# Group-norm tail of a chunked RWKV-7 scan as a stage of its own, its scaling on ScalarE, and 1/|kk|² as a scalar operand in the triangular inverse

## The chip, the cores and the metric

The kernel runs on one core of a Trainium2 chip. The core has five engines that each work through their own list of instructions in order and meet at semaphores: TensorE (PE in the profile, with its weight loads as PEld), VectorE (DVE), ScalarE (ACT), GpSimd (POOL), and SyncE (SP), which here issues most of the DMAs. The metric is the device time of one execution in microseconds (us); a value given for a kernel is the median of its runs.

## What is computed

One layer of a decoder trunk on 1024 tokens of width 1024, all in fp32: an RWKV-7 time mixing, a gated convolution branch and a cross-attention, merged by gates. The change touches the RWKV-7 branch alone. Cut to that branch:

```python
kk = (k * k_k).reshape(B, S, H, N)                 # 16 heads of 64
kk = kk / jnp.maximum(jnp.sqrt(jnp.sum(kk * kk, -1, keepdims=True)), 1e-12)
k = k * (1.0 + (a - 1.0) * k_a)
# for every token t, one state of 64 x 64 for each head:
#   sa = state @ (-kk_t)
#   state = state * decay_t + sa (x) (kk_t * a_t) + v_t (x) k_t
#   y_t = state @ r_t
wkv = wkv7_scan(r, decay, k, v, -kk, kk * a)
mu = jnp.mean(wkv, -1, keepdims=True)              # group norm: one group for each head
var = jnp.mean(jnp.square(wkv - mu), -1, keepdims=True)
wkv = (wkv - mu) * lax.rsqrt(var + 64e-5) * gn_g + gn_b
o_rwkv = wkv + jnp.sum(r * k * r_k, -1, keepdims=True) * v
y_rwkv = (o_rwkv * jax.nn.silu(rwkv_gate)) @ w_proj_rwkv
```

## The kernel before, in words

The scan runs in chunks of 64 tokens. Two heads share the 128 partitions, so there are eight head pairs j, and each goes through two halves e of 512 tokens: 16 **units** (j, e) of eight chunks each. Four generators in the program deal with a unit:

- `prep` makes the scaled operands of the unit (tiles ar and bk), the sums |kk|² (written to a DRAM buffer ssd) and the chunk matrices g, of which the 32 x 32 triangular blocks go to a DRAM buffer ud.
- `sub` inverts those triangles. It loads them as U and |kk|² as rb, takes the reciprocal of rb (L577), multiplies U by it on GpSimd (L581), and puts it on the diagonal of W (L580). Then come 31 steps of two VectorE instructions each: tm = W column x U row (L587) and W += tm (L590). W goes to DRAM (wd, L594) and comes back in another layout as wb (L603). Four transposes (L607) put it into the tile TT, two rounds of small matmuls with a copy by ScalarE behind each (L615, L619, L625, L629) complete the 64 x 64 inverses. TT has one buffer and the next chain reads it.
- `chain` is the recurrence. `g_pre` transposes bk and v (L640, L647) and makes three products with TT and g (L664, L666, L673) that ScalarE copies out (L642, L651, L675, L679, L680). Then for each chunk: a matmul with the state (L709), an add (L710), a matmul for the new state (L717) and two state updates (L720). After each four chunks follow L731, L733, L738 and the statistics of the group norm (bn_stats, L742).
- The **tail** stands at the end of `chain`: six small VectorE instructions on the statistics (L750 to L755), the reciprocal root on GpSimd (L114 and the power L118), subtraction of the mean and product with the root on VectorE (L760, L761), four PE transposes (L766), gain, bonus and gate (L768, L769) and a store (L771).

Beside these, PE makes the big input projections ("dense", L298: 48 matmuls of 128 x 512 for each block of 128 columns), and ScalarE and VectorE split each weight tile in a high and a low part (L123, L124 "wl"). `schedule` says which dense blocks and which generators run together, as a span of the stage for each: while chain (j, 0) runs, sub (j, 1) and prep (j+1, 0) do too. `mix` takes steps of them in turn, and a scheduler in the framework then sets the order of the instructions on each engine. That order, once built, is fixed. After the scan, from about 1040 us on, come convolution, attention and output projections, in which PE has no gaps to speak of.

Of the kernel before, what the change touches and what calls it, by code (L numbers as in the profile page):

```python
# [18 lines left out]
P = 128  # L19
# [4 lines left out]
HS = 512  # L24
C = 64
CPH = HS // C
NG = 4
SUBW = 3
GNW = 1
CHN = 23  # L30
NR = 32 // NG
# [31 lines left out]
def hybrid_kernel(ctx: ExitStack, tc: tile.TileContext, x: bass.AP, mem: bass.AP, wt: bass.AP,  # L63
                  vecs: bass.AP, wup: bass.AP, gfin: bass.AP, out: bass.AP):
    nc = tc.nc
    act, dve, pool, pe = nc.scalar, nc.vector, nc.gpsimd, nc.tensor
# [105 lines left out]
    for j in range(KT):  # L172
        last = j == KT - 1
        schedule.append(([("g", j)] + [fill.pop(0) for _ in range(3)] if last else [("k", j + 1), ("r", j + 1), ("g", j)],
                         [([("chain", j, 0)], 0.0, 1.0), ([("sub", j, 1)], 0.0, 0.9)]
                         + ([] if last else [([("prep", j + 1, 0)], 0.35, 1.0)])))
        schedule.append(([fill.pop(0) for _ in range(2 + last)] + ([] if last else [("v", j + 1)]),
                         [([("chain", j, 1)], 0.0, 1.0)]
                         + ([] if last else [([("sub", j + 1, 0)], 0.0, 0.9), ([("prep", j + 1, 1)], 0.1, 0.9)])))
# [156 lines left out]
    with tc.tile_pool(name="rk", bufs=1, reuse_waits="tile") as rk:  # L336


        def so(par):
            return 0 if par else C  # L340
# [28 lines left out]
        TT = rk.tile([P, 8, C], F32, name="TT")  # L369
# [20 lines left out]
        def fl(ap):  # L390
            return ap.rearrange("p a t -> p (a t)")
# [73 lines left out]
        def g_prep(j, e):  # L465
# [98 lines left out]
        def g_sub(j, e):  # L564
            un = (2 * j + e) % 2
            g = GG[j, e]
            U = rk.tile([NG * 32, 32, 32], F32, name="U", tag="U", bufs=1)
            W = rk.tile([NG * 32, NR, 32], F32, name="W", tag="W")
            rb = rk.tile([NG * 32, 32], F32, name="rb", tag="rb", bufs=2)
            for q in range(NG):  # L570
                ps_ = slice(q * 32, (q + 1) * 32)
                nc.sync.dma_start(out=rb[ps_], in_=ssd[un].rearrange("b h c t -> (b h c) t"))
                nc.sync.dma_start(out=U[ps_], in_=ud[un].rearrange("b i s t -> (b i) s t"))
            pool.memset(W, 0.0)
            yield
            dve.tensor_scalar(out=rb, in0=rb, scalar1=1e-24, scalar2=None, op0=ALU.max)
            dve.reciprocal(out=rb, in_=rb)  # L577
            for q in range(NG):
                ps_ = slice(q * 32, (q + 1) * 32)
                pool.tensor_copy(fl(W[ps_])[:, q::32 + NG], rb[ps_, q::NG])  # L580
            pool.tensor_tensor(out=U, in0=U, in1=rb[:, None, :].broadcast_to([NG * 32, 32, 32]), op=ALU.mult)  # L581
            yield
            tm = rk.tile([NG * 32, max(-(-(i + 1) // NG) * (31 - i) for i in range(31))], F32, name="tm", tag="tm")
            for i in range(31):
                n, m = 31 - i, -(-(i + 1) // NG)
                tv = tm[:, 0:m * n].rearrange("p (a b) -> p a b", b=n)
                dve.tensor_tensor(out=tv, in0=W[:, 0:m, i:i + 1].broadcast_to([NG * 32, m, n]),  # L587
                                  in1=U[:, i:i + 1, i + 1:32].broadcast_to([NG * 32, m, n]), op=ALU.mult)
                wv_ = W[:, 0:m, i + 1:32]
                dve.tensor_tensor(out=wv_, in0=wv_, in1=tv, op=ALU.add)  # L590
                if i % 2:
                    yield
            for q in range(NG):
                nc.sync.dma_start(out=wd[un].rearrange("b i s t -> (b i) s t")[:, q::NG, :],  # L594
                                  in_=W[q * 32:(q + 1) * 32])

            wb = rk.tile([P, 8, 32], F32, name="wb", tag="wb")
            zt = rk.tile([P, 8, 32], F32, name="zt", tag="zt")
            for par in range(2):
                r0 = so(par)  # L600
                for b in range(2):
                    rows = slice(r0 + b * 32, r0 + (b + 1) * 32)
                    nc.sync.dma_start(out=wb[rows], in_=wd[un][b, par::2].rearrange("i s t -> s i t"))  # L603
            for par in range(2):
                for b in range(2):
                    rows = slice(so(par) + b * 32, so(par) + (b + 1) * 32)
                    dve.transpose(out=TT[rows, :, b * 32:(b + 1) * 32], in_=wb[rows])  # L607
            for _ in range(SUBW):
# [74 lines left out]
        def g_chain(j, e):  # L683
# [66 lines left out]
            dve.tensor_tensor(out=mn, in0=stv[:, :, 1], in1=stv[:, :, 4], op=ALU.add)  # L750
            dve.tensor_tensor(out=df, in0=stv[:, :, 1], in1=stv[:, :, 4], op=ALU.subtract)
            dve.tensor_scalar(out=mn, in0=mn, scalar1=0.5, scalar2=None, op0=ALU.mult)
            dve.tensor_tensor(out=vr, in0=stv[:, :, 2], in1=stv[:, :, 5], op=ALU.add)
            dve.tensor_tensor(out=df, in0=df, in1=df, op=ALU.mult)
            dve.scalar_tensor_tensor(out=vr, in0=df, scalar=16.0, in1=vr, op0=ALU.mult, op1=ALU.add)  # L755
            rsqrt(vr, vr, 1.0 / C, GN_EPS)
            for _ in range(GNW):
# [497 lines left out]
```

## Time and profile before

| | us |
|---|---|
| median of 3 runs | 1950.26 (1949.19 to 1952.72) |
| the profiled execution | 1949.77 |
| its span, first to last instruction | 1947.8 |
| PE busy | 1844.5 (95%) |
| DVE busy | 1410.6 (72%) |
| ACT busy | 691.9 (36%) |
| POOL busy | 227.7 (12%) |

Busy times are shares of the whole span, while the kernel has stages with different limits. In the profile's rows of 40 slices, PE is at 9 tenths nearly everywhere, DVE at 7 to 8 tenths in the first half (the scan) and at 9 in the convolution. A matmul's record is longer than the distance to the next matmul, so a busy PE hides small gaps. Instructions of one engine may overlap in their records by some tens of ns where they do not depend on each other.

### The profile page before, as it was taken

The page shows a single profiled execution, that of the slowest core. Times are in us where ns is not written, and L with a number is a line of the kernel's source. Part 1 is how long each engine was busy: PE and PEld are TensorE (multiplying, and loading weights), DVE is VectorE, ACT ScalarE, POOL GpSimd, SP SyncE. Part 2 cuts the span into 40 slices and gives each one's busy share as a digit, 9 for nine tenths or more (in the row PEclk, how much of TensorE's full clock was granted, in tenths as well). Part 3 has the DMA queues.
Part 4 walks back from the last instruction along what each step waited for, and adds up shares of the span by engine and source line. Part 5 has one row for each costly group of instructions (what it writes and reads, how often), then busy time and mean ns, then how long its engine had stood idle before and what let it go on. Part 6 is the DMA issues. An engine that isn't in the chain of part 4 may idle for free.

```text
span 1947.8 us, 30024 instructions
## 1 busy us (share of the span) xinstructions
PE 1844.5 (95%) x11412; PEld 1472.2 (76%) x11412; DVE 1410.6 (72%) x3028; ACT 691.9 (36%) x1303; POOL 227.7 (12%) x311
## 2 busy tenths in 40 slices
PE   6999998999899898998999999999999999899998
PEld 5777776766676676776788888888888788778886
DVE  5667787777878777787735998898999857654423
ACT  6334343433344343343333323131313335432121
POOL 2201111111111112111000000000000223100001
PEclk9999999999999999999999999999999999999999
DMA  4232212222121222212224411112122666785432
GB/s 147 57 99 58 77 35 63 60 56 74 42 83 44 62 63 53 77 42 71 69 72 141 130 54 55 65 59 71 44 76 87 227 199 214 246 283 170 129 130 86
DMA packets 127936, 188.61 MB, mean 97 GB/s; under 512 B 64432, under 2 KB 66608, under 8 KB 127792
## 3 DMA queue, kind: packets, MB, share of 16 engines
q1 hardware_dynamic: 122704, 178.11, 29.8%
q10 hardware_dynamic: 4768, 8.07, 1.1%
q8 instruction: 89, 1.46, 0.3%
q0 software_dynamic: 320, 0.52, 0.1%
q14 instruction: 55, 0.45, 0.1%
HBM read 139.92 MB, written 46.20 MB: 96 GB/s over the span
## 4 chain that ended last, share of the span: by engine, by line
PE 63%; DVE 23%; DMA 4%; issue 4%; ACT 3%; POOL 3%; SPq 0%; DVEq 0%; POOLq 0%; ACTq 0%
PE d L298 41%; PE g L298 5%; PE g L212 4%; DVE W L590 3%; DVE tm L587 3%; PE d L212 2%; DVE s L720 2%; PE g L552 2%; DVE wl L124 2%; DVE sav L710 1%; PE ry L894 1%; POOL vr L118 1%; DVE Y L761 1%; DVE Y L738 1%; PE sas L717 1%
## 5 line engine op out<-in xcount | busy, mean ns | idle before, releaser
L298 PE MATMUL d<-hH,wh 128*128 128x512 f32 x1504 | 607.2, 404 | 2.4 <-ACT lc L383 2.0
L298 PE MATMUL d<-hH,wl 128*128 128x512 f32 x1504 | 603.0, 401 | 0.0
L298 PE MATMUL d<-hL,wh 128*128 128x512 f32 x1504 | 600.1, 399 | 0.0
L298 PEld LDWEIGHTS d<-hH,wl 128*128 128x128 f32 x1504 | 285.0, 189 | 56.9
L298 PEld LDWEIGHTS d<-hH,wh 128*128 128x128 f32 x1504 | 285.3, 190 | 55.8 <-ACT lc L383 2.4
L298 PEld LDWEIGHTS d<-hL,wh 128*128 128x128 f32 x1504 | 285.0, 189 | 53.6
L848 DVE SCALAR_TENSOR_TENSOR ac<-up,wdw,ac 128x1024 f32<-128x1024 f32 x240 | 308.0, 1283 | 11.8 <-ACT ac L845 5.9
L123 ACT CAST wh<-wf 128x1024 fp32r<-128x1024 f32 x137 | 143.6, 1049 | 311.3 <-PE d L298 277.1
L124 DVE TENSOR_TENSOR wl<-wf,wh 128x1024 fp32r<-128x1024 f32 x137 | 177.6, 1296 | 83.8 <-ACT wh L123 83.3
L590 DVE TENSOR_TENSOR W<-W,tm 128x60 f32<-128x60 f32 (+24 forms) x496 | 112.3, 226 | 10.0
L587 DVE TENSOR_TENSOR tm<-W,U 128x60 f32<-128x60 f32 (+24 forms) x496 | 107.7, 217 | 11.1
L713 ACT ACTIVATE sp<-s,pc 128x128 f32<-128x128 f32 x120 | 48.3, 402 | 174.8 <-DVE s L720 137.6
L717 PEld LDWEIGHTS sas<-sav,tk 128*128 128x128 f32 x240 | 38.5, 188 | 67.7 <-DVE sav L710 49.4
L717 PE MATMUL sas<-sav,tk 128*128 128x128 f32 x240 | 54.2, 307 | 34.3 <-DVE sav L710 32.6
L720 DVE SCALAR_TENSOR_TENSOR s<-sas,pc,sp 64x64 f32<-64x64 f32 x240 | 67.6, 282 | 21.5 <-PE sas L717 16.1
L298 PE MATMUL g<-oH,wh 128*128 128x512 f32 x192 | 76.3, 398 | 5.3 <-ACT wh L123 5.3
L298 PE MATMUL g<-oH,wl 128*128 128x512 f32 x192 | 76.2, 397 | 2.1 <-DVE wl L124 2.1
L298 PE MATMUL g<-oL,wh 128*128 128x512 f32 x192 | 75.8, 395 | 0.0
L298 PE MATMUL d<-oL,wh 128*128 128x512 f32 x192 | 75.2, 392 | 0.0
L298 PE MATMUL d<-oH,wl 128*128 128x512 f32 x192 | 75.2, 392 | 0.0
L298 PE MATMUL d<-oH,wh 128*128 128x512 f32 x192 | 75.2, 392 | 0.0
L710 DVE TENSOR_TENSOR sav<-ry,Y 64x128 f32<-64x128 f32 x128 | 36.8, 287 | 43.7 <-ACT Y L675 26.8
(301 smaller groups left out, 2910.6 us busy)
## 6 DMA issues: line engine op xcount, KB each, us to landing
wf<-in_wt_dram SPq DMA_DIRECT2D x137, 512.0 KB
g_d<-gt SPq DMA_DIRECT2D x48, 256.0 KB
U<-ud SPq DMA_DIRECT2D x64, 128.0 KB
nxt<-in_x_dram SPq DMA_DIRECT2D x8, 512.0 KB
o_rwkv_d<-o SPq DMA_DIRECT2D x16, 256.0 KB
cv_d<-ac SPq DMA_DIRECT2D x8, 512.0 KB
o_mem_d<-om SPq DMA_DIRECT2D x16, 256.0 KB
xs<-cv_d SPq DMA_DIRECT2D x8, 512.0 KB
```

Of the source, the lines that this page charges most:

```text
L123: act.copy(hi, src)
L124: (eng or dve).tensor_tensor(out=lo, in0=src, in1=hi.bitcast(F32), op=ALU.subtract)
L212: pe.matmul(po, lhsT=l, rhs=r, start=(i == 0), stop=(i == n - 1))
L298: pe.matmul(po, lhsT=l[:, ks_], rhs=r[:, k, sl], start=(n == 0), stop=(n == 3 * KT - 1))
L552: pe.matmul(gps[hh][:, cc * P:(cc + 1) * P], lhsT=fl(bk[rows, c, :, :]), rhs=fl(ar[rows, c, :, :]), start=True, stop=True)
L587: dve.tensor_tensor(out=tv, in0=W[:, 0:m, i:i + 1].broadcast_to([NG * 32, m, n]), in1=U[:, i:i + 1, i + 1:32].broadcast_to([NG * 32, m, n] ...
L590: dve.tensor_tensor(out=wv_, in0=wv_, in1=tv, op=ALU.add)
L710: dve.tensor_tensor(out=sav[own, cc, :], in0=ry[own, cs], in1=Y[own, c // 2, :], op=ALU.add)
L713: act.activation(sp, S0, AF.Copy, scale=pc[:, c:c + 1])
L717: pe.matmul(sn[:, 0:P], lhsT=tk[:, cc, :], rhs=sav[:, cc, :], start=True, stop=True)
L720: dve.scalar_tensor_tensor(out=S1[vsl, vsl], in0=sn[vsl, vsl], scalar=pc[vsl, c:c + 1], in1=sp[vsl, vsl], op0=ALU.mult, op1=ALU.add)
L848: dve.scalar_tensor_tensor(out=ac, in0=up[:, tap:tap + S], scalar=wdw[:, tap * 8 + j:tap * 8 + j + 1], in1=ac, op0=ALU.mult, op1=ALU.add)
```

## The change

The tail leaves `chain` and becomes a generator `g_tail` that the schedule puts beside the *next* unit's chain, in the first half of its stage. The small arithmetic on the statistics moves from VectorE to GpSimd (eight small instructions beside the root), and the normalisation from two VectorE instructions over 128 x 512 to eight ScalarE instructions over 128 x 64 with a scale and a bias for each partition. Y, st and bv get two buffers, bk goes from three to two.

In `sub`, the diagonal of W is set to one by GpSimd, U stays as loaded, and 1/|kk|² enters each step as a scalar operand for each partition; one product at the end scales all of W. W gets two buffers. wb and zt now lie in U's buffer. One transpose over 128 partitions takes the place of four over 32, with two ScalarE copies for the part that it puts in the wrong column.

```diff
-    W = rk.tile([NG * 32, NR, 32], F32, name="W", tag="W")
+    W = rk.tile([NG * 32, NR, 32], F32, name="W", tag="W", bufs=2)
...
-        pool.tensor_copy(fl(W[ps_])[:, q::32 + NG], rb[ps_, q::NG])
-    pool.tensor_tensor(out=U, in0=U, in1=rb[:, None, :].broadcast_to([NG * 32, 32, 32]), op=ALU.mult)
+        pool.memset(fl(W[q * 32:(q + 1) * 32])[:, q::32 + NG], 1.0)
...
-        dve.tensor_tensor(out=tv, in0=W[...], in1=U[...], op=ALU.mult)
+        dve.scalar_tensor_tensor(out=tv, in0=W[...], scalar=rb[:, i:i + 1], in1=U[...], op0=ALU.mult, op1=ALU.mult)
...
+    dve.tensor_tensor(out=W, in0=W, in1=rb[:, None, :].broadcast_to([NG * 32, NR, 32]), op=ALU.mult)
...
-    wb = rk.tile([P, 8, 32], F32, name="wb", tag="wb")
-    zt = rk.tile([P, 8, 32], F32, name="zt", tag="zt")
+    wb, zt = U[:, 0:8, :], U[:, 8:16, :]
...
-            dve.transpose(out=TT[rows, :, b * 32:(b + 1) * 32], in_=wb[rows])     # 4 times
+    dve.transpose(out=TT[:, :, 0:32], in_=wb)
+        act.copy(TT[r1:r1 + 32, :, 32:C], TT[r1:r1 + 32, :, 0:32])               # 2 times
...
+def g_tail(j, e):
+    Y, st, bv = ENDS.pop((j, e))
...
-    dve.tensor_tensor(...)  six small ones on mn, df, vr
+    pool.tensor_tensor(...), pool.tensor_scalar(...)  eight small ones on mn, df, vr
     rsqrt(vr, vr, 1.0 / C, GN_EPS)
...
-    dve.tensor_tensor(out=yv, in0=yv, in1=mn[:, :, None].broadcast_to([P, n2, C]), op=ALU.subtract)
-    dve.tensor_tensor(out=yv, in0=yv, in1=vr[:, :, None].broadcast_to([P, n2, C]), op=ALU.mult)
+    for i in range(n2):
+        act.activation(yv[:, i, :], yv[:, i, :], AF.Identity, scale=vr[:, i:i + 1], bias=mn[:, i:i + 1])
```

Three places in the order of instructions, all around the start of chain (3, 1), show what this moves. Line numbers are those of the kernel that is shown. **ScalarE at the start of the chain**, before: zt and TT close the previous `sub`, then come the copies of `g_pre` (tk, sav, Y, tk, g).

```order
L629 COPY TT<-tr 32x8x32 x2
L733 COPY Y<-tr 128x256
L123 CAST wh<-wf 128x1024
L427 ACTIVATE sg<-d 128x512
L436 ACTIVATE gt<-d 128x512
L642 COPY tk<-tr 128x512
L651 COPY sav<-tr 64x2x128 x2
L675 COPY Y<-tr 128x256
L679 COPY tk<-g 64x2x128
```

And now, with the normalisation of the unit that has just ended (L768):

```order
L629 COPY TT<-tr 32x8x32 x2
L735 COPY Y<-tr 128x256
L643 COPY tk<-tr 128x512
L652 COPY sav<-tr 64x2x128 x2
L768 ACTIVATE Y<-Y,mn,vr 128x64 x3
L676 COPY Y<-tr 128x256
L680 COPY tk<-g 64x2x128
```

Three of the eight scalings of the old unit now stand ahead of the Y copy that the new chain's first add needs.

**VectorE at the start of the chain**, before:

```order
L760 TENSOR_TENSOR Y<-Y,mn 128x512
L428 SCALAR_TENSOR_TENSOR sg<-sg,d 128x512
L761 TENSOR_TENSOR Y<-Y,vr 128x512
L768 SCALAR_TENSOR_TENSOR o<-tr,vec,bv 128x512
L769 SCALAR_TENSOR_TENSOR o<-o,vec,sg 128x512
L710 TENSOR_TENSOR sav<-ry,Y 64x128
L587 TENSOR_TENSOR tm<-W,U 128x31
L590 TENSOR_TENSOR W<-W,tm 128x31
```

And now:

```order
L744 BN_STATS st<-Y 128x6 x4
L712 TENSOR_TENSOR sav<-ry,Y 64x128
L722 SCALAR_TENSOR_TENSOR s_0_405<-sas,pc,sp 64x64 x2
L488 TENSOR_SCALAR lw<-lw 128x512
L700 TENSOR_TENSOR bv<-g,v 128x512
L494 SCALAR_TENSOR_TENSOR lw<-rmask,lw 128x512
L712 TENSOR_TENSOR sav<-ry,Y 64x128
L586 SCALAR_TENSOR_TENSOR tm<-W,rb,U 128x31
L590 TENSOR_TENSOR W<-W,tm 128x31
```

The tail is gone from here, and the first of the 31 inverse steps stands behind the first state update where it stood ahead of it. (In the sub beside an even chain, (j, 0), the first step stood ahead even of the chain's first add.)

**VectorE between the last inverse step and the transposes**, in the sub beside chain (3, 0), whose result chain (3, 1) needs, before:

```order
L590 TENSOR_TENSOR W<-W,tm 128x8
L124 TENSOR_TENSOR wl<-wf,wh 128x1024
L720 SCALAR_TENSOR_TENSOR s_0_405<-sas,pc,sp 64x64 x2
L576 TENSOR_SCALAR rb<-rb 128x32
L124 TENSOR_TENSOR hsl<-rs,hsh 128x512
L710 TENSOR_TENSOR sav<-ry,Y 64x128
L577 RECIPROCAL rb<-rb 128x32
L555 TENSOR_TENSOR g<-g,cmask_384 128x512 x2
L720 SCALAR_TENSOR_TENSOR s_1_406<-sas,pc,sp 64x64 x2
L428 SCALAR_TENSOR_TENSOR sg<-sg,d 128x512
L607 STREAM_TRANSPOSE TT<-wb 32x8x32 x3
```

And now:

```order
L590 TENSOR_TENSOR W<-W,tm 128x8
L593 TENSOR_TENSOR W<-W,rb 128x256
L124 TENSOR_TENSOR wl<-wf,wh 128x1024
L429 SCALAR_TENSOR_TENSOR sg<-sg,d 128x512
L604 STREAM_TRANSPOSE TT<-U 128x8x32
```

The state updates, the masks of g (L555) and the head sums that stood behind the last step now stand ahead of it, between the steps.

## Rows read from the trace of the kernel before

**Rows 1.** Windows: us; busy (instructions) of PE, PEld, DVE, ACT, POOL; clock, DMA, GB/s.
```profile
520.80:636.30 115.50, 105.86 (x892) 80.53 (x890) 90.03 (x282) 45.35 (x98) 16.93 (x26) 1.00 0.22 59
1100.00:1200.00 100.00, 100.00 (x463) 83.44 (x462) 87.94 (x80) 25.98 (x33) 5.33 (x4) 1.00 0.22 69
```

**Rows 2.** Waits of PE over the span: us in total, times, longest.
```profile
PE sas L717 <- DVE sav L710: 32.6, 43, 1.9
PE tr L766 <- DVE Y L761: 19.1, 6, 3.2
```

**Rows 3.** Timeline, one tail: start us, us, instruction [idle before <-releaser].
```profile
529.55 0.69 DVE L760 TENSOR_TENSOR Y<-Y,mn 128x512 f32<-128x512 f32 x1
...
529.79 0.50 POOL L114 TENSOR_SCALAR vr<-vr 128x8 f32<-128x8 f32 x1 [11.90 <-DVE vr L755]
530.37 1.64 POOL L118 TENSOR_TENSOR vr<-vr,nhalf 128x8 f32<-128x8 f32 x1
531.98 2.34 POOL L581 TENSOR_TENSOR U<-U,rb 128x1024 f32<-128x1024 f32 x1
...
532.05 2.82 DVE L761 TENSOR_TENSOR Y<-Y,vr 128x512 f32<-128x512 f32 x1 [1.10 <-POOL vr L118]
...
535.01 0.63 PE L766 MATMUL tr<-ident,Y 128*128 128x128 f32 x4 [3.16 <-DVE Y L761]
```

**Rows 4.** Timeline of PE: the first, three in a row, the last L625 of sixteen.
```profile
127.16 0.69 PE L625 MATMUL tr<-zt,wb 32*32 32x32 f32 x32
...
523.52 0.69 PE L625 MATMUL tr<-zt,wb 32*32 32x32 f32 x32
...
584.61 0.69 PE L625 MATMUL tr<-zt,wb 32*32 32x32 f32 x32
...
637.39 0.69 PE L625 MATMUL tr<-zt,wb 32*32 32x32 f32 x32
...
980.64 0.69 PE L625 MATMUL tr<-zt,wb 32*32 32x32 f32 x32
```

**Rows 5.** Timeline of DVE: first and last step of one sub; second and last of the next.
```profile
540.72 0.19 DVE L587 TENSOR_TENSOR tm<-W,U 128x31 f32<-128x31 f32 x1
...
570.90 0.17 DVE L590 TENSOR_TENSOR W<-W,tm 128x8 f32<-128x8 f32 x1
...
594.46 0.18 DVE L587 TENSOR_TENSOR tm<-W,U 128x30 f32<-128x30 f32 x1
...
626.17 0.17 DVE L590 TENSOR_TENSOR W<-W,tm 128x8 f32<-128x8 f32 x1
```

**Rows 6.** Timeline of DVE: last inverse step, and transposes that wait for the data.
```profile
396.79 0.17 DVE L590 TENSOR_TENSOR W<-W,tm 128x8 f32<-128x8 f32 x1
...
405.24 0.90 DVE L607 STREAM_TRANSPOSE TT<-wb 32x256 f32<-32x256 f32 x2 [1.00 <-DMA wb<-wd]
```

**Rows 7.** Timeline: the start of chain (3, 1) on three engines.
```profile
527.29 0.60 DVE L742 BATCH_NORM_STATS2 st<-Y 128x6 f32<-128x64 f32 x4
...
539.99 0.37 ACT L675 COPY Y<-tr 128x256 f32<-128x256 f32 x1 [0.82 <-ACT sav L651]
...
540.84 0.46 PE L717 MATMUL sas<-sav,tk 128*128 128x128 f32 x2
```

**Rows 8.** Groups by line, 60 to 1040 us: busy us, mean ns | idle before.
```profile
L768 DVE SCALAR_TENSOR_TENSOR o<-tr,vec,bv 128x512 f32<-128x512 f32 x16 | 12.0, 750 | 7.0 <-PE tr L766 7.0
L698 DVE TENSOR_TENSOR bv<-g,v 128x512 f32<-128x512 f32 x16 | 11.1, 691 | 9.6 <-PE g L462 9.2
L555 DVE TENSOR_TENSOR g<-g,cmask 128x512 f32<-128x512 f32 x64 | 42.3, 687 | 19.0 <-PE g L552 18.6
L720 DVE SCALAR_TENSOR_TENSOR s<-sas,pc,sp 64x64 f32<-64x64 f32 x240 | 67.6, 282 | 21.5 <-PE sas L717 16.1
L713 ACT ACTIVATE sp<-s,pc 128x128 f32<-128x128 f32 x120 | 48.3, 402 | 174.8 <-DVE s L720 137.6 <-DVE s L687 36.5
L114 POOL TENSOR_SCALAR vr<-vr 128x8 f32<-128x8 f32 x16 | 4.9, 308 | 210.4 <-DVE vr L755 210.4
```

More of the change, by code (lines that the diff above doesn't have):

```diff
@@ L28 @@
 SUBW = 3
-GNW = 1
+GNW = 2
 CHN = 23
@@ L175, in hybrid_kernel @@
                          [([("chain", j, 0)], 0.0, 1.0), ([("sub", j, 1)], 0.0, 0.9)]
+                         + ([([("tail", j - 1, 1)], 0.0, 0.5)] if j else [])
                          + ([] if last else [([("prep", j + 1, 0)], 0.35, 1.0)])))
         schedule.append(([fill.pop(0) for _ in range(2 + last)] + ([] if last else [("v", j + 1)]),
-                         [([("chain", j, 1)], 0.0, 1.0)]
+                         [([("chain", j, 1)] + [("tail", j, 1)] * last, 0.0, 1.0), ([("tail", j, 0)], 0.0, 0.5)]
                          + ([] if last else [([("sub", j + 1, 0)], 0.0, 0.9), ([("prep", j + 1, 1)], 0.1, 0.9)])))
@@ L574, in g_sub @@
             pool.memset(W, 0.0)
+            for q in range(NG):
+                pool.memset(fl(W[q * 32:(q + 1) * 32])[:, q::32 + NG], 1.0)
             yield
@@ L586, in g_sub @@
                 tv = tm[:, 0:m * n].rearrange("p (a b) -> p a b", b=n)
-                dve.tensor_tensor(out=tv, in0=W[:, 0:m, i:i + 1].broadcast_to([NG * 32, m, n]),
-                                  in1=U[:, i:i + 1, i + 1:32].broadcast_to([NG * 32, m, n]), op=ALU.mult)
+                dve.scalar_tensor_tensor(out=tv, in0=W[:, 0:m, i:i + 1].broadcast_to([NG * 32, m, n]),
+                                         scalar=rb[:, i:i + 1], in1=U[:, i:i + 1, i + 1:32].broadcast_to([NG * 32, m, n]),
+                                         op0=ALU.mult, op1=ALU.mult)
                 wv_ = W[:, 0:m, i + 1:32]
@@ L603, in g_sub @@
                     nc.sync.dma_start(out=wb[rows], in_=wd[un][b, par::2].rearrange("i s t -> s i t"))
+            dve.transpose(out=TT[:, :, 0:32], in_=wb)
             for par in range(2):
-                for b in range(2):
-                    rows = slice(so(par) + b * 32, so(par) + (b + 1) * 32)
-                    dve.transpose(out=TT[rows, :, b * 32:(b + 1) * 32], in_=wb[rows])
+                r1 = so(par) + 32
+                act.copy(TT[r1:r1 + 32, :, 32:C], TT[r1:r1 + 32, :, 0:32])
             for _ in range(SUBW):
@@ L635, in hybrid_kernel @@
         state = [0]
+        ENDS = {}
         def g_pre(j, e, q, g, bk, v, Y):
@@ L749, in g_chain @@
             df = rk.tile([P, n2], F32, name="df", tag="df", bufs=1)
[L750 to L755, printed above, removed]
+            pool.tensor_tensor(out=mn, in0=stv[:, :, 1], in1=stv[:, :, 4], op=ALU.add)
+            pool.tensor_tensor(out=df, in0=stv[:, :, 1], in1=stv[:, :, 4], op=ALU.subtract)
+            pool.tensor_tensor(out=vr, in0=stv[:, :, 2], in1=stv[:, :, 5], op=ALU.add)
+            pool.tensor_tensor(out=df, in0=df, in1=df, op=ALU.mult)
+            pool.tensor_scalar(out=df, in0=df, scalar1=16.0, scalar2=None, op0=ALU.mult)
+            pool.tensor_tensor(out=vr, in0=vr, in1=df, op=ALU.add)
             rsqrt(vr, vr, 1.0 / C, GN_EPS)
+            pool.tensor_scalar(out=mn, in0=mn, scalar1=-0.5, scalar2=None, op0=ALU.mult)
+            pool.tensor_tensor(out=mn, in0=mn, in1=vr, op=ALU.mult)
             for _ in range(GNW):
@@ L759, in g_chain @@
             yv = Y.rearrange("p c (h v) -> p (c h) v", h=2)
-            dve.tensor_tensor(out=yv, in0=yv, in1=mn[:, :, None].broadcast_to([P, n2, C]), op=ALU.subtract)
-            dve.tensor_tensor(out=yv, in0=yv, in1=vr[:, :, None].broadcast_to([P, n2, C]), op=ALU.mult)
-            for _ in range(GNW):
-                yield
+            for i in range(n2):
+                act.activation(yv[:, i, :], yv[:, i, :], AF.Identity, scale=vr[:, i:i + 1], bias=mn[:, i:i + 1])
+                if i % 4 == 3:
+                    yield
             ytp = bank("tr")
@@ L775, in jobs @@
             return seq(*[tile_job(*a_) for a_ in lst])
-        n_steps = {"dense": 12, "prep": 13, "sub": 20 + SUBW, "chain": CHN + 2 * GNW}
-        make = {"prep": g_prep, "sub": g_sub, "chain": g_chain}
+        n_steps = {"dense": 12, "prep": 13, "sub": 20 + SUBW, "chain": CHN, "tail": 3 + GNW}
+        make = {"prep": g_prep, "sub": g_sub, "chain": g_chain, "tail": g_tail}
         for lst, work in schedule:
```

11 lines of the change are left out of this document (5 added, 6 removed).

## The prediction

> **What bounds the kernel now.** I read the windows first: 115.5 us in the middle of the scan (two units) and 100 us after it [rows 1]. After the scan PE does 463 instructions in 100 us with no gap, nearly all dense matmuls, so one costs 100/463 = 0.216 us. In the scan PE is busy 105.9 of 115.5 us, VectorE 90.0. Neither is full, so the stage is held by waits. Of PE's waits by releaser [rows 2] two matter: 19.1 us on the normalisation (six of 3.2 us at most), and 32.6 us in 43 short waits for the first add of a chunk.
>
> The timeline of one tail shows the first kind [rows 3]: L761 starts late, behind the root (1.64 us), takes 2.82 us beside the 2.34 us product of U on GpSimd, and PE stands 3.16 us ahead of the transposes L766, with the dense matmuls and the next chain's start queued behind. That is what the change removes.
>
> But what is this hidden by? A unit is a loop: inverse done (L625), chain starts, VectorE runs the next 31 steps, W goes through DRAM, L625 again. I count the scan in these intervals. From the first L625 to the last are 980.64 - 127.16 = 853.5 us, 15 of them, 56.9 each [rows 4]. Two in a row, 523.52 to 584.61 (61.1) and to 637.39 (52.8), split with the steps [rows 5] into three legs:
>
> - A, from L625 to the steps: 17.2 (540.72) in the first, 9.85 (594.46, the second step) in the second.
> - B, the steps to 571.07 and 626.34: 30.35 and 31.9.
> - C, from there to the next L625: 13.5 and 11.05.
>
> VectorE is back to back in B, so an instruction put there lengthens it, and its order is fixed. I take these legs for the bound, and ask what the change does to each.
>
> **Leg A.** The tail leaves the path, but something enters it. The statistics end 4.4 us after L625 (527.29 + 0.60 - 523.52, [rows 7]). Then GpSimd does eight small instructions, L114 and the power. For the small ones the nearest row is L114, 0.31 on the mean [rows 8] and 0.50 in the tail shown [rows 3]; a VectorE instruction as small, a bn_stats, takes 0.15 [rows 7], which is the lower end. With 0.31: 9 x 0.31 + 1.64 = 4.4, so they end at 8.8. As the order shows, three scalings of the old unit stand on ScalarE ahead of L675, which the new chain's first add needs. A 128 x 128 ScalarE instruction takes 0.40 [rows 8], which bounds the 128 x 64 one from above, half of that from below; I take 0.33, so 9.8. From the start of L675 to L717 are 0.85 [rows 7]: 10.7, with some 0.2 of semaphores 10.9. VectorE's first step now stands behind the first two state updates (2 x 0.28) and two large instructions or the second chunk's add: another 2.1. First step at 13.0 in both kinds. The first kind gains 4.2; the second, where the steps started ahead of the chain, loses 3.1. The ends for the small ones, 0.15 and 0.50, move A by -1.4 and +1.7.
>
> Does the small work on GpSimd disturb VectorE? L760, two operands from SBUF, took 0.69 while L114 ran beside it (0.50 in place of 0.31); L761 took 2.82 beside the 128 x 1024 product [rows 3]. So I take nothing for it.
>
> The Trainium skill, "GPSIMD Engine Reference", section 1 Specifications, states that GpSimd shares its SBUF interface with VectorE and contends with VectorE instructions that have two SBUF inputs. The large product agrees (2.82), the small L114 doesn't (0.69); by the rule the sum would be that of the fourth rival below, by the row it stays as it is.
>
> **Leg B.** Each step takes a scalar operand: the pointer form costs 0.750 against 0.691 of the plain product at the same size [rows 8], 0.06 each, 31 of them 1.9. The product that scales W is half of a 128 x 512 one, about 0.4. And the instructions that lay behind the last step or in the tail's place now stand between the steps. By the order of the first kind: two adds (0.28 each, as L720), L768 and L769 (0.75 each), two masks (0.69 each), two blends of the 0.75 form, less L698 and one of half a microsecond: 3.7. The sum is 6.0; neighbours that don't depend overlap by some tens of ns, so 5.5, and B is 36.0. In the second kind: four masks, two gates (0.69 each), one split (1.4), some small ones, less three blends and L698: 3.2; with 1.9 and 0.4 it is 5.5, and the first step, which now belongs to B, adds 0.4. B is 37.6. Lower end: VectorE absorbs the moved work in waits that the sum doesn't see, and only the 2.3 of the new product form stay: 32.6 and 34.5.
>
> **Leg C.** W's round trip through DRAM is 405.24 - 396.96 = 8.3 us [rows 6]. Behind it come one transpose (half of the 0.90 of two, 0.45), a round of small matmuls and a ScalarE copy: 10.5. PE's own queue has some 80 dense matmuls ahead of that round, 80 x 0.216 = 17.3, which began late since PE now waits at the chain's start; they may end a microsecond later. I take 11.0 for both. Little VectorE work is left here, so what left C is no gain beyond 2.5 in the first kind and nothing in the second. Two buffers for W only free GpSimd, which waits for nothing that anyone needs. U is loaded right after L625, since the wb in it is then free, and that is long ahead of 13.0.
>
> **The sum.** First kind 13.0 + 36.0 + 11.0 = 60.0; second 13.0 + 37.6 + 11.0 = 61.6. The order gives the first five intervals no such load, I leave them at 57; the last has a loop a fifth shorter, 52. Nine between at 60.6, a little under the mean of both: 285 + 545 + 52 = 882, +29. Behind the last L625 there are 51 fewer dense matmuls, -11.0, less 3 for the last unit's tail that nothing covers: -8. Two terms were taken at their full size, B's moved work and A's second kind; I take off 2. So +19 on the profiled 1949.8, which stands 0.5 under the median: **1969**.
>
> **The rivals.**
>
> - *PE is the bound.* The legs have slack that I don't see, VectorE takes its moved work in waits, and PE gets back its 19.1 us [rows 2] and the 11.0 at the end: 1920; with half of the 32.6 us of short waits 1904. For it: VectorE's total falls (L760, L761 and six small instructions against 2.3 + 0.4), and 90 of 115.5 leaves room. Against it: B is back to back. 0.28.
> - *Nothing net.* A's gain of 4.2 and C's of 2.5 in the first kind pay for B; intervals of 57.4 and 8 off the end: 1949 (1946 to 1953). 0.14.
> - *The chain waits for GpSimd longer.* The one place is the start of a chain, where three scalings stand ahead of L675. If the small instructions cost the 0.50 of rows 3, A grows by 1.7, over 15 units 25: 1994. It decides from about 0.4 each. Against it: VectorE has nothing to do then. 0.11.
> - *The small work on GpSimd slows VectorE* as the product did to L761, by 2.1 in 2.3 us. Then up to 4.4 us come back on VectorE for each unit, 15 x 4.4 = 66: 2035. Against it: L760 beside L114, and that VectorE waits then. 0.02.
> - *The change doesn't do what it says*, and the transposes still wait: L766 now stands behind the new chain's first products, some 5 us after the scalings, so no; inside the forecast.
>
> **How the numbers follow.** Forecast (1955 to 1985) 0.45, PE-bound 0.28, nothing 0.14, GpSimd's waits 0.11, its hold on VectorE 0.02. 0.2%, about 4 us, is what a measurement of this kernel can tell from no change. Faster 0.28, same 0.14, slower 0.58. The range, 1922 to 1996, leaves out the lower half of the PE-bound case and the far end above. The forecast's own range is 1955 to 1985.
>
> **What would show it.** L625 to L625 near 60 us in the middle of the scan against 57; the first step 13 us after L625; 36 us and more from first to last step; PE waiting no longer for the normalisation at L766, but ahead of L717 at the start of a chain and ahead of L615 for the round trip; ScalarE waiting for GpSimd right ahead of the scalings. If the first step comes by 10 us, or B stays at 32, the forecast is wrong and the PE-bound case right.

## The result, and the profile after

The changed kernel takes 1995.7 us (median of 4 runs, 1993.7 to 1997.3), the kernel before 1951.4: a ratio of 1.0241 with an interval of 1.0229 to 1.0253, 44 us slower. The forecast was slower, by 19. The time lies at the upper end of the range, and the loss is more than twice the forecast's. In the runs below, one execution of the kernel before, beside e13, took 2727.6 us at a granted clock of 0.61 and is left out of the ratio, and of e6 there is one execution alone.

The busy times of the changed kernel, from its page:

```profile
PE 1881.4 (94%) x11412; PEld 1512.6 (76%) x11412; DVE 1347.0 (67%) x2868; ACT 747.2 (37%) x1463; POOL 206.9 (10%) x423
```

VectorE has 64 us less to do than before (1410.6) and GpSimd 21 less, ScalarE 55 more. The time was not lost by work. Windows of the same 120 us in the middle of the scan, before and then after (us, busy us of PE, PEld, DVE, ACT, POOL with instructions, granted clock, DMA):

```profile
640.00:760.00 120.00, 110.28 (x867) 84.23 (x867) 93.25 (x294) 47.12 (x100) 17.76 (x28) 0.99 0.22 62
```

```profile
640.00:760.00 120.00, 109.98 (x818) 85.26 (x814) 71.58 (x231) 49.96 (x114) 12.96 (x38) 0.91 0.20 57
```

VectorE is busy for 22 us less, TensorE as long as before with fewer instructions, at a lower clock. Now the places that answer to [rows 4], the matmuls L625 of the changed kernel (start us, us): the first, three in a row, the last.

```profile
126.03 0.69 PE L625 MATMUL tr<-U 32*32 32x32 f32 x32
...
602.25 0.69 PE L625 MATMUL tr<-U 32*32 32x32 f32 x32
...
666.31 0.69 PE L625 MATMUL tr<-U 32*32 32x32 f32 x32
...
731.93 0.69 PE L625 MATMUL tr<-U 32*32 32x32 f32 x32
...
1036.78 0.69 PE L625 MATMUL tr<-U 32*32 32x32 f32 x32
```

From the first to the last are 910.8 us in place of 853.5: 57.3 lost here. Behind the last 958.7 are left of the span of 1995.5, before 967.2 of 1947.8: 8.5 won there. So the whole loss is in the fifteen intervals of the scan, as the prediction counted them.

TensorE's time in this whole stretch, from the first L625 to the last, before and then after:

```profile
127.16:980.64 853.48, 787.17 (x6317) 599.74 (x6317) 655.86 (x2054) 335.58 (x718) 121.95 (x183) 0.99 0.22 61
126.03:1036.78 910.75, 832.18 (x6368) 646.96 (x6368) 595.38 (x1915) 386.39 (x864) 100.06 (x275) 0.96 0.21 58
```

It is idle for 12.3 us more (78.6 for 66.3) and busy for 45.0 more. The 51 dense matmuls that the stretch has more are 11 us of this, at 0.216 each. And TensorE is busy for 75 us at a granted clock of 0.50, where it was 17: half of such time is lost, so 29 us more. This says where TensorE's time went; what would come back with the clock kept up, no run shows.

How one interval starts, from 666.31 on, answers to [rows 3, 7]:

```profile
670.83 0.21 POOL L754 TENSOR_TENSOR mn<-st 128x8 f32<-128x8 f32 x1 [12.14 <-DVE st L744]
...
672.84 1.67 POOL L118 TENSOR_TENSOR vr<-vr,nhalf 128x8 f32<-128x8 f32 x1
...
674.59 0.21 POOL L763 TENSOR_TENSOR mn<-mn,vr 128x8 f32<-128x8 f32 x1
674.83 1.10 ACT L768 ACTIVATE Y<-Y,mn,vr 128x64 f32<-128x64 f32 x3 [2.82 <-POOL mn L763]
675.95 0.37 ACT L676 COPY Y<-tr 128x256 f32<-128x256 f32 x1
...
676.38 0.44 PE L641 MATMUL tr<-ident,bk 128*128 128x128 f32 x2 [2.92 <-ACT Y L676]
...
676.80 0.46 PE L719 MATMUL sas<-sav,tk 128*128 128x128 f32 x2
...
677.30 0.77 PE L299 MATMUL d<-hH,wl 128*128 128x512 f32 x1
677.88 0.63 PE L299 MATMUL d<-hH,wh 128*128 128x512 f32 x1
...
680.00 0.24 DVE L586 SCALAR_TENSOR_TENSOR tm<-W,rb,U 128x31 f32<-128x31 f32 x1
```

GpSimd's small work ends 8.5 us after L625, ScalarE waits 2.82 us for it with the old unit's three scalings and the new chain's copy L676 behind, and TensorE stands 2.92 us at L641, which needs the bank (of PSUM, the memory that TensorE writes to) that this copy frees. Over the span these stalls are now TensorE's largest wait, and the tail's transposes (L773 here), 19.1 us in [rows 2], wait for 1.4:

```profile
PE tr L641 <- ACT Y L676: 32.2, 11, 3.0
PE ry L711 <- DVE s L722: 15.6, 19, 2.0
...
PE sas L719 <- DVE sav L712: 12.7, 18, 1.6
...
PE tr L773 <- ACT Y L768: 1.4, 4, 0.4
```

The stall at the tail is gone, and one about as long (2.92 us for 3.16) stands a few instructions on.

### The profile page after: what moved, and what is told of

The parts are those of the page before. It is cut to its first block, busy times and chain, and to the rows that moved or that the text cites. A ratio compares the mean times of both kernels' runs of the same rounds, so it can differ in the third digit from the quotient of the medians.

```text
span 1995.5 us, 30108 instructions
## 1 busy us (share of the span) xinstructions
PE 1881.4 (94%) x11412; PEld 1512.6 (76%) x11412; DVE 1347.0 (67%) x2868; ACT 747.2 (37%) x1463; POOL 206.9 (10%) x423
## 4 chain that ended last, share of the span: by engine, by line
PE 66%; DVE 19%; ACT 4%; POOL 4%; DMA 4%; issue 3%; DVEq 0%; POOLq 0%; SPq 0%; ACTq 0%
PE d L299 44%; PE g L299 5%; PE g L213 4%; DVE tm L586 3%; DVE W L590 2%; PE d L213 2%; DVE s L722 2%; PE g L553 2%; POOL vr L118 1%; DMA ost<-o_rwkv_d 1%; PE ry L901 1%; DVE wl L124 1%; PE sas L719 1%; PE ry L213 1%; DVE Y L740 1%
## 5 line engine op out<-in xcount | busy, mean ns | idle before, releaser
L299 PEld LDWEIGHTS d<-hH,wh 128*128 128x128 f32 x1504 | 287.5, 191 | 65.1 <-ACT gt L437 3.0
L299 PEld LDWEIGHTS d<-hL,wh 128*128 128x128 f32 x1504 | 286.9, 191 | 56.2
L124 DVE TENSOR_TENSOR wl<-wf,wh 128x1024 fp32r<-128x1024 f32 x137 | 170.7, 1246 | 122.6 <-ACT wh L123 117.6
L586 DVE SCALAR_TENSOR_TENSOR tm<-W,rb,U 128x60 f32<-128x60 f32 (+24 forms) x496 | 134.6, 271 | 10.6 <-DMA U<-ud 2.6
L590 DVE TENSOR_TENSOR W<-W,tm 128x60 f32<-128x60 f32 (+24 forms) x496 | 105.9, 214 | 7.5
L711 PEld LDWEIGHTS ry<-s,ar 128*128 128x128 f32 x256 | 48.2, 204 | 36.8 <-DVE s L722 28.2
L719 PEld LDWEIGHTS sas<-sav,tk 128*128 128x128 f32 x240 | 43.8, 208 | 39.1 <-DVE sav L712 24.6
```

What stands on the lines that cost most here:

```text
L124: (eng or dve).tensor_tensor(out=lo, in0=src, in1=hi.bitcast(F32), op=ALU.subtract)
L299: pe.matmul(po, lhsT=l[:, ks_], rhs=r[:, k, sl], start=(n == 0), stop=(n == 3 * KT - 1))
L586: dve.scalar_tensor_tensor(out=tv, in0=W[:, 0:m, i:i + 1].broadcast_to([NG * 32, m, n]), scalar=rb[:, i:i + 1], in1=U[:, i:i + 1, i + 1:32 ...
L711: pe.matmul(ry[:, cs], lhsT=fl(ar[:, c, :, :]), rhs=S0, start=True, stop=True)
L719: pe.matmul(sn[:, 0:P], lhsT=tk[:, cc, :], rhs=sav[:, cc, :], start=True, stop=True)
```

## The experiments

In the table, A, B and C are the legs of the prediction, as means over the nine intervals in the middle (the sixth to the fourteenth). A is counted to the very first step, so the kernel before has 5.6 and 18.8 in its two kinds. "Lost" is leg by leg the time times one less the granted clock, summed. The product of W that closes the new inverse (0.46) lies in C here, while the prediction counted it in B.

| kernel | us | ratio (95%) | interval | A | B | C | lost to the clock |
|---|---|---|---|---|---|---|---|
| before | 1951 | | 58.1 | 12.7 | 32.9 | 12.5 | 0.8 |
| changed | 1995.7 | 1.0241 (1.0229 to 1.0253) | 62.9 | 13.4 | 36.3 | 13.2 | 3.6 |
| e1 scalings behind the copy | 1986.9 | 1.0172 (1.0147 to 1.0196) | 62.3 | 11.3 | 37.2 | 13.8 | 3.8 |
| e2 useless matmuls | 1993.7 | 1.0212 (1.0191 to 1.0233) | 61.8 | 12.6 | 36.3 | 12.9 | 1.9 |
| e3 tail alone | 1975.4 | 1.0124 (1.0102 to 1.0146) | 58.5 | 16.2 | 29.9 | 12.3 | 1.9 |
| e4 inverse alone | 1971.4 | 1.0098 (1.0080 to 1.0116) | 58.9 | 11.6 | 34.7 | 12.6 | 1.5 |
| e5 inverse alone, plain product | 1995.3 | 1.0241 (1.0226 to 1.0256) | 60.4 | 14.3 | 33.5 | 12.7 | 2.5 |
| e6 fewer dense matmuls | 2034.3 | one execution | 65.1 | 14.0 | 35.8 | 15.3 | 6.6 |
| e7 tail alone, scalings behind | 1937.8 | 0.9942 (0.9924 to 0.9961) | 56.4 | 13.9 | 29.6 | 12.9 | 0.9 |
| e8 the same, GpSimd helps | 1958.7 | 1.0052 (1.0036 to 1.0069) | 57.6 | 14.3 | 30.8 | 12.5 | 1.3 |
| e9 changed, buffers of their own | 1958.7 | 1.0039 (1.0025 to 1.0054) | 57.4 | 9.6 | 34.7 | 13.1 | 2.3 |
| e10 before, shared buffer | 2001.5 | 1.0269 (1.0248 to 1.0290) | 61.4 | 16.5 | 32.8 | 12.1 | 3.4 |
| e11 as e9, scalings behind | 1915.1 | 0.9823 (0.9803 to 0.9842) | 55.3 | 8.5 | 33.4 | 13.4 | 0.4 |
| e12 as e7, U first | 1902.6 | 0.9754 (0.9738 to 0.9770) | 53.8 | 10.7 | 30.9 | 12.2 | 0.0 |
| e13 dense matmuls behind L615 | 2000.4 | 1.0262 (1.0239 to 1.0286) | 60.9 | 10.7 | 36.6 | 13.6 | 3.4 |

**The two theories of the start.** Theory 1 was the stall shown above and the half clock behind it, theory 2 VectorE's work between the steps. The first edit ties the scalings to the copy (a dependency that only sets the order on ScalarE):

```diff
-                act.activation(yv[:, i, :], yv[:, i, :], AF.Identity, scale=..., bias=...)
+                with tc.issue_after(ycopy):        # the last copy of zv into Y
+                    act.activation(yv[:, i, :], yv[:, i, :], AF.Identity, scale=..., bias=...)
```

> The changed kernel with one edit: the eight scalings of the old unit are tied behind the copy that brings the first products of the new chain into Y, so that three of them no longer stand ahead of it on ScalarE. Theory 1 (the 3 us for which TensorE stands at the chain's start, and the half clock that follows, push the dense matmuls that the next inverse waits for): the 2.9 us stalls shrink to under 1.5 us, the granted clock in the scan goes from 0.96 to 0.99, the mean interval from L625 to L625 from 60.7 to 57 to 58.5, time 1940 to 1960. Theory 2 (VectorE's work between the steps is the bound): clock or not, intervals stay at 60 or more, time 1980 to 1996.

1986.9: nearer to theory 2. Leg A lost 2.1, but B and C took 1.5 of it back, the granted clock in the scan stayed at 0.96, and TensorE's waits only moved on, to the next links of the chain:

```profile
PE ry L712 <- DVE s L723: 18.6, 22, 2.0
PE sas L720 <- ACT tk L681: 18.0, 9, 2.6
```

The second keeps TensorE busy in the stall:

```diff
+            sn0 = bank("sas")
...                                                # tied behind the first products, the next transposes behind it
+            for _ in range(8):
+                pe.matmul(sn0[:, P:HS], lhsT=bones, rhs=lox[:, 0, 0:3 * P], start=True, stop=True)
```

> The changed kernel with useless work added: eight 128x384 matmuls into an unused part of a bank, for each chain, put where TensorE stands and waits at its start. About 8 x 0.16 x 16 = 21 us more for TensorE, nothing for the other engines. Theory 1: the clock stays at 0.98 or more in the scan, and the time FALLS to 1965 to 1985 in spite of it. Theory 2: no fall, 1994 to 2017.

1993.7, within the spread of the changed kernel: 8 useless matmuls a unit cost nothing, the clock lost 1.9 us an interval and not 3.6, and the intervals fell by 1.1 of the 4.8 that they had grown by. So theory 1 as put down, that the time follows once the stall is filled, fell. What the clock costs is not settled by it: the granted clock of the scan rose to 0.97 and not to 0.98 or more, and the useless matmuls (some 20 us for TensorE) weigh about as much as the clock that came back.

**The two parts apart.**

```diff
 # e3: g_sub as before, all else as changed (st in one buffer, for room)
 # e4: g_sub as changed, all else as before
```

> The new tail alone (a generator of its own beside the next chain, scalings on ScalarE, small work on GpSimd), with the inverse as it was before: scaled U, no scalar operand, four transposes, wb and zt tiles of their own. Theory 1: the scalings ahead of the chain's copy and the wait are there, so most of the loss too: 1975 to 1990. Theory 2: VectorE has 2.3 us less between the steps than in the changed kernel and no tail: 1935 to 1955.

> The new inverse alone (scalar operand in each step, a product at the end, one transpose and two copies, two buffers for W, wb and zt in U's buffer), with the tail at the end of the chain as before. Theory 1: no new wait at the chain's start; 31 x 0.06 + 0.4 = 2.3 us more for VectorE a unit, 2.4 less for GpSimd beside the tail's product: 1940 to 1965. Theory 2: 16 x 2.3 = 37 us more: 1980 to 1992.

Each costs about half: 24 and 20 us, with a sum of 44. In the first, B is shorter by 3.0, the tail's work on VectorE, and A longer by 3.5: in every second chain all eight scalings stand ahead of the copy there, in most of the others four. In the second, TensorE stands at the old tail's transposes for 51 us and not 19 [rows 2], all but one of the sixteen times:

```profile
PE tr L765 <- DVE Y L760: 51.0, 15, 7.1
```

**The scalar operand.** The fifth is the fourth with U scaled on GpSimd and the plain product, so that what is new is the one transpose, W's second buffer and the buffer that wb and zt share with U.

```diff
-                dve.scalar_tensor_tensor(out=tv, in0=W[...], scalar=rb[:, i:i + 1], in1=U[...], op0=ALU.mult, op1=ALU.mult)
+                dve.tensor_tensor(out=tv, in0=W[...], in1=U[...], op=ALU.mult)
-            dve.tensor_tensor(out=W, in0=W, in1=rb[...], op=ALU.mult)
+            pool.tensor_tensor(out=U, in0=U, in1=rb[...], op=ALU.mult)     # ahead of the steps, with the diagonal
```

> The new inverse alone, as before, but without the scalar operand: U is scaled and the diagonal set on GpSimd as in the kernel before, each step is the plain product again and the product at the end is gone; one transpose, two buffers for W, wb and zt in U's buffer stay. If VectorE's 31 x 0.055 + 0.43 = 2.1 us a unit are the loss of that part (VectorE's work between the steps is the bound): 16 x 2.1 = 34 less at most, 1937 to 1953, B 2 us shorter. If the loss is the order (steps behind the chain's first add, the tail's stall of up to 7 us ahead of the transposes) or the late load into the shared buffer: 1965 to 1980, B as it is.

1995.3, 24 us slower than with the scalar. B is 1.2 us shorter, but A 2.7 longer. So the scalar operand wins time, 24 us, and something else in the new inverse loses twice as much. VectorE's load between the steps, theory 2, is not it either.

**Less work for TensorE.**

```diff
+            three = ((wh, rh), (wh, rl), (wl, rh)) if idx < T_M0 or idx >= T_PR else ((wh, rh), (wl, rh))
...
-                for l, r in ((wh, rh), (wh, rl), (wl, rh)):
+                for l, r in three:
```

> The changed kernel with a third of the dense matmuls of the memory gate's blocks left out (the product of the low part of the input with the weights' high part; the values of these gates are then less exact). Two such blocks run beside each chain (j, 1) and none beside (j, 0), up to j = 6: 32 x 0.216 = 6.9 us less for TensorE in every second interval. If TensorE's work is the bound, those intervals fall by 5 to 7, from 62.4 to 56. If the loop of VectorE and the DRAM trip is the bound and TensorE only delays the end of leg C, they fall by the wait of L615 there, 2 to 3 us, to about 60, and the others stay at 63 to 64.

The kernel leaves out a third of the products of the memory gate's blocks, whose values are then less exact. 2034.3 in its one execution: slower, which neither case expected. With a fifth of the dense work gone from every second stage (32 of 144 matmuls), the intervals grew from 62.3 to 64.8 there and from 63.6 to 65.6 in the others. A window of the stage (us, busy us of the engines, clock, DMA):

```profile
400.00:640.00 240.00, 207.51 (x1449) 157.23 (x1448) 149.07 (x472) 89.82 (x198) 24.07 (x68) 0.89 0.20 55
```

The granted clock there is 0.89, where the changed kernel has 0.96 and e12 1.00. Over the scan, 270 dense matmuls fewer take 58 us off TensorE, and the lower clock takes as much from it again (99 us lost for 41). So a shorter list of matmuls alone did not make the loop shorter, but this test does not clear TensorE's time of a part in the loss. Leg C grew by 2.1 on the mean. The transposes stand on VectorE behind a weight's low part, which waits for the cast on ScalarE, which waits for a dense block:

```profile
761.86 1.23 DVE L124 TENSOR_TENSOR wl<-wf,wh 128x1024 fp32r<-128x1024 f32 x1 [4.83 <-ACT wh L123]
...
763.73 0.44 DVE L606 STREAM_TRANSPOSE TT<-U 128x256 f32<-128x256 f32 x1
```

**The new tail in its place.** The seventh is the third with the edit of the first.

> The new tail alone, with the eight scalings tied behind the copy of the new chain's first products (the edit of the first experiment on the third's kernel). There six scalings and more stand ahead of that copy in every second chain and leg A is 18.7 to 19.9 us. If that is what the new tail costs, A falls by 3 to 6 and the mean interval from 58.4 to 55 or 56: 1930 to 1955. If leg A is held by something else (the chain of small work for the chain's start), 1965 to 1980.

1937.8: 37.6 us less than without it, and 0.6% faster than the kernel before. So the tail's loss was its three to eight scalings on ScalarE ahead of the new chain's first copy. One long wait is left at the first step:

```profile
DVE tm L588 <- POOL U L582: 45.1, 7, 6.5
```

The eighth gives GpSimd the low parts of the head sums as well:

```diff
-            split_sb(t, hi, lo)
+            split_sb(t, hi, lo, eng=pool)
```

> As the one before it, and the low parts for the two head sums of a unit (128 x 512, 0.72 us each on VectorE) are made by GpSimd. If VectorE's work between the steps is the bound, B falls by up to 1.4 us a unit, 10 to 22 us under the one before it. If not, the same time as that within 6 us, or more by GpSimd's 1.5 us each on the path of the head sums.

1958.7, 21 us more than the seventh, and B did not fall (30.8 for 29.6). Less load on VectorE did not shorten that loop. GpSimd takes 1.30 to 1.37 for the subtraction and VectorE 0.69 to 0.71; that this stands on the loop's path is argued, not shown.

**The shared buffer.** The ninth takes it out of the changed kernel, the tenth puts it alone into the kernel before.

```diff
 # e9, in the changed kernel (W and st in one buffer each, for room); e10 is the reverse in the kernel before
-            wb, zt = U[:, 0:8, :], U[:, 8:16, :]
+            wb = rk.tile([P, 8, 32], F32, name="wb", tag="wb")
+            zt = rk.tile([P, 8, 32], F32, name="zt", tag="zt")
```

> The changed kernel with wb and zt in tiles of their own again, so that the next unit's U no longer waits for L625 to be loaded (W and st in one buffer, for room). The scalar operand, the product at the end, the one transpose and the new tail stay. If the shared buffer is what costs, by putting the steps behind the start of the chain and the dense matmuls in a block ahead of L615: the block there falls from 54 to 57 matmuls to 13 to 39, as the order shows, and the time to 1955 to 1975, B still 2 us longer than before. If the scalar operand and the moved work between the steps cost: 1985 to 2000.

> The kernel before with one edit: wb and zt lie in U's buffer, as in the change. Nothing is added on any engine. If the late load of U is free (it lands some 5 us after L625, ahead of the first step in every second unit): 1945 to 1957. If it takes the early start from the steps of the other units (5.5 us after L625 before): U lands at 4 to 5, GpSimd's product 2.4, behind the tail's root: first step at 11 to 13 in place of 5.5, intervals of 52.8 go to 58 to 60, time 1980 to 2000.

1958.7: 37 us of the changed kernel's 44 are gone. And 2001.5: an edit of two lines, which adds no instruction to any engine, costs the kernel before 50 us. In its trace the loads of U are issued right behind L625 (L624 there), and GpSimd can take U only behind the tail's root:

```profile
610.99 0.69 PE L624 MATMUL tr<-U 32*32 32x32 f32 x32
...
611.77 1.71 SPq L573 DMA_DIRECT2D U<-ud  x4
...
617.07 1.65 POOL L118 TENSOR_TENSOR vr<-vr,nhalf 128x8 f32<-128x8 f32 x1
618.68 2.34 POOL L581 TENSOR_TENSOR U<-U,rb 128x1024 f32<-128x1024 f32 x1
618.75 2.82 DVE L760 TENSOR_TENSOR Y<-Y,vr 128x512 f32<-128x512 f32 x1 [2.12 <-POOL vr L118]
...
624.29 0.18 DVE L587 TENSOR_TENSOR tm<-W,U 128x31 f32<-128x31 f32 x1
```

The first step comes 13.3 us after L625. The same place in the kernel before, where U had been scaled ahead of L625 (584.61 in [rows 4]) and the first step came 5.55 us after it:

```profile
581.94 2.38 POOL L581 TENSOR_TENSOR U<-U,rb 128x1024 f32<-128x1024 f32 x1 [4.87 <-DMA U<-ud]
...
590.16 0.18 DVE L587 TENSOR_TENSOR tm<-W,U 128x31 f32<-128x31 f32 x1
```

Every second interval goes from 52.8 to 61.1, and the others stay (61.7, 62.3 before): the one edit, seen alone. Part of its way is the clock: the intervals lose 3.4 us to it, 0.8 before.

**What the change gives without its two obstacles.** The eleventh is the ninth with the scalings tied behind the copy.

> The ninth experiment's kernel with the scalings tied behind the chain's first copy: new tail, scalar operand, nothing shared. Beside the seventh (the same with U scaled on GpSimd, 1937.8) it shows the scalar operand alone: VectorE 2.1 us more a unit between the steps, against 2.4 us of GpSimd and a wait of up to 6.5 us for it in every second unit there. If VectorE decides: 1950 to 1970. If the wait for GpSimd does: 1915 to 1935.

1915.1: 36 us faster than the kernel before. Against the seventh the scalar operand (with the one transpose) is worth 23 us, through A (8.5 for 13.9), at 3.8 us more of B. The twelfth keeps U scaled on GpSimd, ahead of the tail's small work:

```diff
+            with tc.issue_after(uprod):            # the product of U, as last written
                 pool.tensor_tensor(out=mn, in0=stv[:, :, 1], in1=stv[:, :, 4], op=ALU.add)   # and df, vr
 # schedule: tails in 0.1 to 0.6 of the stage, not 0.0 to 0.5
```

> A version that may beat both: the seventh experiment's kernel, where VectorE's first step waits 45 us in all for GpSimd's product of U, which stands behind the tail's small work and its root. Here the tail's small work is tied behind that product, and the tail starts a tenth of the stage later. If that wait holds leg A, the first steps of every second unit go from 12.5 us after L625 to 6 to 8, and the time from 1937.8 to 1900 to 1925. If TensorE holds the loop there (it is idle for 4 of 56 us), 1930 to 1940.

1902.6, 2.5% faster than the kernel before: better than both. The first step of every second unit comes 6.0 us after L625, no clock is lost, and the product of U lies ahead of L625 (L628 there) again:

```profile
558.83 2.39 POOL L584 TENSOR_TENSOR U<-U,rb 128x1024 f32<-128x1024 f32 x1 [6.87 <-DMA U<-ud]
559.19 0.69 PE L628 MATMUL tr<-zt,wb 32*32 32x32 f32 x32
...
565.15 0.18 DVE L590 TENSOR_TENSOR tm<-W,U 128x31 f32<-128x31 f32 x1
565.32 0.21 POOL L759 TENSOR_TENSOR mn<-st 128x8 f32<-128x8 f32 x1 [4.09 <-DVE v L386]
```

**Leg C.** The last question was why C is 13.2 and not 11.0. In the changed kernel (the end of the interval from 666.31):

```profile
718.59 0.17 DVE L590 TENSOR_TENSOR W<-W,tm 128x8 f32<-128x8 f32 x1
...
718.79 0.43 DVE L593 TENSOR_TENSOR W<-W,rb 128x256 f32<-128x256 f32 x1
...
727.24 0.45 DVE L604 STREAM_TRANSPOSE TT<-U 128x256 f32<-128x256 f32 x1 [0.49 <-DMA U<-wd]
...
729.72 0.69 PE L615 MATMUL tr<-TT,g 32*32 32x32 f32 x32
```

L615 starts 2.0 us after its data, at the end of a gapless block of dense matmuls. The thirteenth ties the dense matmuls that the program writes behind L615 to it, so that none stands right ahead of it and 40, not 15 to 20, are among TensorE's first 110 matmuls of the next chain in the trace.

```diff
+                    with tc.issue_after(lastz):    # the last matmul of L615's round, once there is one
                         pe.matmul(po, lhsT=l[:, ks_], rhs=r[:, k, sl], start=..., stop=...)
```

> The changed kernel with the dense matmuls that the program writes behind the first small matmuls of the inverse (L615) tied behind them: none stands right ahead of L615 (54 to 57 before), and 50 in the first 110 instructions of the next chain (15 before). The shared buffer, the scalar operand, the new tail and the work of every engine are as in the changed kernel. If TensorE's order is what makes leg C 13.2 and not 11.3, and what lets the clock fall at the bare chain start: granted clock 0.99 in the scan, C 11 to 11.5, time 1950 to 1975. If the block only filled time that the loop takes anyway, TensorE now waits for the DRAM trip with nothing to do: 1990 to 2030.

2000.4. L615 follows its data at once, but the data come later (the transpose starts 10 to 12.5 us after the last step: in some units behind masks and adds on VectorE, in others behind the loads of wb, which SP issues among other transfers), and C is 13.6. That fits a block which only filled time that the loop takes anyway. It doesn't show it, as the edit moved more than the block: all eight scalings, not three, now stand ahead of the new chain's first copy, which starts 16 to 19 us after L625 and not at 9.7, and the granted clock of the scan stays at 0.96. So the edit shows that clearing L615's queue alone does not shorten C; what would, stays open.

## Why the prediction was half right

The view held: the loss is in the intervals, the sign was right, and the end came out at -8.5 for -8. The terms:

- **What bounds the kernel.** The prediction took the loop of inverse and chain, and not TensorE. With the same matmuls, edits that let the steps or the chain start earlier gave 35 to 44 us, each against the kernel that it edits (e7, e9, e11, e12), and one that makes the steps late cost 50 (e10); so the order around the loop decides. That TensorE's time has no part in it is not shown. The prediction has no term for the clock: 41 us of the scan are lost to it, 8.5 before, and each of those four edits also lowered that loss (to 0.0 in e12). How much of the 44 us is the clock's own stays open.
- **Leg A** was right in its steps: GpSimd ended 8.5 us after L625 (8.8 forecast; its small instructions took 0.20 to 0.24 and not 0.31), the three scalings 1.10 (1.0), L719 started at 10.5 (10.9), the first step at 13.7 in the interval shown and 13.4 on the mean, 14.2 and 12.5 in the two kinds (13.0 for both).
- **Leg B** was right: 35.4 and 37.4 in the two kinds, 35.8 and 37.8 with the product of W that the prediction counted in it, for 36.0 and 37.6 (its own terms add up to 35.9 and 37.8). The scalar operand costs what was worked out from [rows 8]: a step's product 271 ns now, 217 before, so 0.054 and not 0.06.
- **Leg C is the step that failed.** Forecast 11.0 for both kinds; measured, from the end of the product of W, 12.3 and 13.2, that is 15 us in nine intervals. The trip through DRAM with the transpose came as forecast (8.80 on the mean, 8.75 forecast), and from L615 to L625 it took 1.88 (1.75). The term that was too small is TensorE's queue ahead of L615, "they may end a microsecond later", which the sum has at 0.5: L615 stood 2.03 behind its data. And the prediction let 2.5 us of the first kind's 13.5 go because VectorE's work had left; with the product counted in, 0.7 went there, and the second kind's 11.1 grew to 13.7. C is 12.6 to 13.8 in every kernel with the new inverse (15.3 in e6), 12.1 to 12.9 with the old one. Why it does not come down to 11 stays open: without the queue the data came later (e13).
- **The first five intervals** were left at 57, and they took 58.6 (56.2 before): the loop of the first went from 47.9 to 54.8. That is 8 us more. Taking off 2 us for full-size terms had no ground either. With leg C's 15 and 4 of leg A these make some 29 us, which is what the forecast is short of.
- **The place that it passed over.** "U is loaded right after L625 ... long ahead of 13.0" priced the shared buffer at nothing. In the changed order U did land ahead of the first step; but the buffer is why the order had become so: with tiles of their own again the first step of the second kind comes at 5.0 and not at 12.5 (e9). Alone it costs 50 us (e10), and the same steps that it made late stood in the prediction as a matter of order, 3.1 us of leg A in the second kind with what goes with it in B. So the sum held most of it under another name, and the text named the wrong owner: it put the loss down to the moved work and the scalar operand between the steps, while the scalar operand wins 24 us (e5 against e4).
- **The rivals.** PE-bound and nothing net did not come, and GpSimd's small work took 0.20 to 0.24, so the third, which needed 0.4, was not the way; that its 1994 lies beside the measured time is chance. The fourth did not show: e11 and e12 have that work too. The Trainium skill's rule ("GPSIMD Engine Reference", section 1 Specifications) on the shared SBUF interface is seen again at the large product alone: 2.82 for L760 beside L581 in e10.

By single edits, in this order, the way from one kernel to the other is: shared buffer +50, one transpose and W's second buffer -6, scalar operand -24, new tail +24. In another order the shares differ: taken out of the changed kernel, the shared buffer is worth 37.

## What to carry over

A buffer given to a second user makes the next load wait for that user: ask of every tile that is merged what was loaded early before, and which first step stood on it. Work that is moved off a stall to a less busy engine still stands in that engine's order; look at what is queued behind it there, and tie it behind what the critical loop needs. When a kernel is bound by a loop, sum the loop's legs; an engine's freed time off them (64 us of VectorE here) may buy nothing. And read the granted clock beside the legs: here it was lower than before in every kernel whose intervals grew.

## What the runs showed of the hardware

TensorE's clock was granted at 0.50 (1.2 GHz of 2.4) for 17 of the 65.6 us of the interval from 666.31. Windows of 2 us there: the stall at full clock; half of it soon after the next matmuls; full again in a window that is busy for 0.88; half once more, from 684.0 to 697.6, also in windows with no idle time; then full.

```profile
674.00:676.00 2.00, 0.00 (x0) 0.00 (x0) 0.00 (x0) 1.15 (x4) 0.71 (x2) 1.00 0.00 0
...
678.00:680.00 2.00, 2.00 (x6) 1.52 (x5) 1.03 (x2) 1.03 (x3) 0.00 (x0) 0.50 0.00 0
...
682.00:684.00 2.00, 0.88 (x18) 0.55 (x17) 1.93 (x6) 1.89 (x5) 1.66 (x3) 1.00 0.00 0
...
688.00:690.00 2.00, 2.00 (x12) 1.54 (x10) 0.86 (x4) 0.84 (x3) 0.00 (x0) 0.50 0.01 2
...
698.00:700.00 2.00, 2.00 (x21) 1.54 (x20) 1.94 (x8) 0.00 (x0) 0.00 (x0) 1.00 0.00 0
```

With a third of some blocks' matmuls left out (e6) the granted clock over the run was 0.944, with all of them 0.975, and with useless ones added (e2) 0.983. That leaving them out made it fall is not shown, since e6 has one execution and another order of instructions; behind the scan (1130 to 2032 us) it was 1.00, as in the changed kernel.
